# Splitting weights into high and low parts 1024 columns at a time instead of 512

## The chip, the cores and the metric

The kernel runs on one core of a Trainium2 chip. The metric is the device time of one execution in microseconds (us). Engines are named as in the profile: PE is TensorE (PEld its weight load), DVE is VectorE, ACT is ScalarE, POOL is GpSimd, SP is SyncE, on whose queue the loads of weights are issued.

## The reference, cut to what matters

Two blocks follow each other on 256 tokens of width 2048, all in float32. The first has two layers, each with a projection of the normed input into the columns of four mixers (gated linear attention, forgetting, differential and block attention), the mixers, and a projection back. The second has one layer with a modulated input projection for tokens and for a context, recurrent scans in both directions (RWKV-7 and a gated delta rule), a gated merge, and an MLP with squared ReLU. Nearly all of the multiplications are products of 256 tokens with large weights:

```python
def hybrid_layer(x, ...):                       # first block, two layers
    h = rms_norm(x, norm_g)
    p = split_columns(jnp.einsum("bsd,de->bse", h, w_in))
    ...                                         # four mixers
    return x + jnp.einsum("bse,ed->bsd", mixed, w_out)

def trunk_layer(x, ctx, c, c_ctx, ...):         # second block, one layer
    mod = jax.nn.silu(c) @ mod_w + mod_b
    h = modulate(rms_norm_2(x, norm1_w), sh1, sc1)
    p = h @ in_w
    ...                                         # scans, for tokens and context
    x = x + g1 * merge_branches(ya, yb, pg, up_a, up_b, out_w)
    x = x + g2 * squared_relu_mlp(modulate(rms_norm_2(x, norm2_w), sh2, sc2), mlp_w1, mlp_w2)

def squared_relu_mlp(h, w1, w2):
    return jnp.square(jax.nn.relu(h @ w1)) @ w2
```

## The kernel before, in words

Every float32 operand of a large product is split into a high part, rounded to float32r, and a low part, which is the rest. A product is then three matmuls: high weights with the high part of the activations (L171), high weights with the low part (L172), and low weights with the high part (L173). Where the two parts of the activations lie side by side (512 columns, in the output projection and in the second product of the MLP) the first two are one matmul (L166), and L167 is the one with the low weights. L203 to L205 are the same for outputs that stand as [token, feature].

Weights come from HBM as blocks of 128 x 2048. `load_w` loads a block as two tiles `wr` of 1024 columns, one DMA of 512 KB each, on SP's queue; there are three such buffers (WR). `pieces` makes of each 512 columns a high part `wh` by a copy on ACT (L230) and a low part `wl` by a subtraction on DVE (L231). There are five buffers of each kind (WH). A buffer of `wh` or `wl` becomes free when PE has done its last matmul with it, and a buffer of `wr` when the second subtraction from it is done. One `wr` holds eight slices of 128 columns, each the weights of one step over k; PE takes them in the order in which they were made.

The program is written stage by stage. A scheduler at build time lays out the order of the instructions of each engine; nothing is reordered when it runs. The loads and the split of weights are put AHEAD = 400 instructions before their place, so that they stand among other work on ACT and DVE. The stages of a run, by time, are: the first layer (to about 600 us) beside the modulation of the second block, whose steps use DVE (L901, L906), ACT (L911) and POOL (L912); the second layer (to about 1200); the scans, two at a time, with the projections of the second block between them (to about 2500); the merge and the start of the MLP (to about 2900); the rest of the MLP (to 3440); and the last norm. In the first two stages the softmax of the mixers stands on DVE too: L578 takes logits from PSUM, L529 row maxima, L426 to L430 rotate queries and keys.

Of the kernel before, what the change touches and what calls it, by code (L numbers as in the profile page):

```python
# [10 lines left out]
F32R = mybir.dt.float32r  # L11
# [5 lines left out]
PSUM = bass.MemoryType.PSUM  # L17
# [7 lines left out]
# how many instructions ahead of their place the operands of a projection are made  # L25
AHEAD = 400
# buffers of weights as they come, and of their parts
WR, WH = 3, 5
# buffers of 1 and 2 KB of the scans
N1, N2, NM = 6, 5, 4  # L30
# steps by which one scan runs ahead of the next
LEAD = 8
# banks of the projections, and of each of two scans
PP, S0, S1 = 3, 3, 2
# by how many instructions the scans go before the projections beside them
SCANS = 4000
# buffers of 2 KB of the scans, and of 4 KB of their inversions
NN, NL = 3, 3
# steps of the modulation by group of columns, for its first third and after
R0, R1, R2 = 3, 2, 3  # L40
# by how many instructions the parts of x go before their place
XO = (800, 300, 240, 200)
# groups of the modulation before the MLP; in the MLP, steps by pair of columns, from which pair on
MQ, MR, MS = 20, 3, 2
# the last product: on GpSimd or VectorE, and which rows
OUTS = ((0, 0, 1), (1, 12, 14), (0, 1, 3), (0, 3, 6), (0, 6, 9), (1, 14, 16), (0, 9, 12))
# how many of the context's activations are made early, buffers for the others
# [3 lines left out]
def bc(ap, n, axis):  # L51
    """ap with an axis of length n and step 0 put in at `axis`."""
    l = [list(x) for x in ap.ap]
    l.insert(axis, [0, n])
    return bass.AP(tensor=ap.tensor, offset=ap.offset, ap=l)


class Env:
    def __init__(self, tc, ctx):
# [8 lines left out]
        # which of two scans is being traced: each has its own banks  # L68
# [5 lines left out]
    def scr(self, shape, name):  # L74
        """A short-lived [128, up to 512]."""
        n = int(np.prod(shape[1:]))
        w, k = (512, 5) if n > 256 else (256, 3) if n > 64 else (64, 4)
        t = self.kp.tile([128, w], F32, name=name, tag="zsh" if w == 256 else f"scr{w}", bufs=k)[:shape[0], :n]
        return t.rearrange("p (a b) -> p a b", a=shape[1]) if len(shape) == 3 else t
# [10 lines left out]
    def consts(self):  # L90
# [7 lines left out]
        # tri[s, t] = 1 for s <= t, then ones: the running sums of two blocks of 128  # L98
        self.tri = c("tri", [128, 256])
        g.affine_select(self.tri, o, pattern=[[1, 256]], compare_op=ALU.is_ge, fill=0.0, base=0, channel_multiplier=-1)  # L100
        # fold[p, m] = 1 for p equal to m modulo 32
# [4 lines left out]
        # causal masks, 0 or -1e30: [q, key] of a block on the diagonal, and of the second row of blocks  # L106
# [4 lines left out]
    def level_masks(self):  # L111
        """uint8 masks [s, t] of pairs that a halving level joins: s in the left half, t in the
        right half of one block of 2b; the last is the diagonal."""
        nc, g = self.nc, self.nc.gpsimd
        self.lm = {}
        for b in (16, 8, 4, 2, 1):
            nb = 64 // b
            m = self.scr([128, 128], "lmf")
            # t in the right half of block j: start from ones on [j, half, i], zero on the left half
            mv = m.rearrange("p (n h i) -> p n h i", n=nb, h=2)  # L120
            g.memset(m, 0.0)
            # keep where 0 <= j*2b + b - 1 - s  (s <= last of left half) and s >= j*2b
# [10 lines left out]
    def load_w(self, dram):  # L133
        """One block of weights [128, 2048]; its high and low parts in four pieces each."""
        nc = self.nc
        out = []
        with self.tc.high_priority(offset=AHEAD):
            for j in range(2):
                w = self.wp.tile([128, 1024], F32, name="wr", tag="wr", bufs=WR)
                nc.sync.dma_start(w, dram[:, j * 1024:(j + 1) * 1024])  # L140
                for q in range(2):
                    out.append(self.pieces(w[:, q * 512:(q + 1) * 512]))
        return out

    def proj_t(self, h, dram, blocks, eat, nk=NK, w=T):
        """Two times 128 outputs, [feature, w columns of h], one after the other: eat(f, psum) for each."""
        n = 0
        for b in blocks:
            for hi, lo in self.load_w(dram[b]):
                for a in range(4):  # L150
# [10 lines left out]
    def mm3(self, o, hi, lo, h, k, nk):  # L161
        """o += what k adds; of 512 columns, the second half gets high times low."""
# [15 lines left out]
    def proj_k(self, h, dram, blocks, eat):  # L178
        """Two times 128 outputs, [feature, token], side by side, so that h is free by k as it ends:
        eat(f, psum); blocks of 1024 rows and 256 columns."""  # L180
        p = [self.pp()[:, :T] for _ in range(2)]
        k = 0
        for b in blocks:
            for hi, lo in self.load_w(dram[b]):
                for n in range(4):
                    sl = slice(n * 128, (n + 1) * 128)
                    self.mm3(p[n % 2], hi[:, sl], lo[:, sl], h, k + n // 2, NK)
                k += 2
# [4 lines left out]
    def proj_n(self, h, dram, tiles, eat, nk=NK):  # L193
        """512 outputs, [token, feature]: eat(block of tokens, psum)."""
# [4 lines left out]
        for ti in tiles:  # L199
            for hi, wlo in self.load_w(dram[ti]):  # L200
                for b in range(2):
                    x, xl = (h[i][:, k, b * 128:(b + 1) * 128] for i in range(2))
                    mm(p[b], x, hi, start=k == 0, stop=False)  # L203
                    mm(p[b], x, wlo, start=False, stop=False)
                    mm(p[b], xl, hi, start=False, stop=k == nk - 1)  # L205
                k += 1
# [4 lines left out]
    def proj_s(self, x, g, dram):  # L211
        """32 outputs of x * g, [feature, token]; dram [128, 16 x 32], g by feature. The sums over the k
        equal modulo 4 go to four groups of rows."""
# [12 lines left out]
    def pieces(self, sl):  # L226
        """(high, low) of weights [128, 512]."""
        hi = self.wp.tile([128, 512], F32R, name="wh", tag="wh", bufs=WH)
        lo = self.wp.tile([128, 512], F32R, name="wl", tag="wl", bufs=WH)
# [5 lines left out]
    def rsqrt(self, out, x, shape, tag, mult=1.0, eps=0.0):  # L235
        """out = (x * mult + eps) ** -0.5 by Newton's steps on VectorE."""
# [9 lines left out]
    def log1p_exp_neg_abs(self, out, x, shape, tag):  # L246
        """out = log(1 + exp(-|x|)); x in SBUF."""
# [34 lines left out]
    def total(self, acc, bank=None):  # L282
        """Sums over the partitions of acc [128, 256] by token, [128, 2]."""
# [10 lines left out]
    def rows(self, col, out=None, bank=None):  # L294
        """What is by token, [128, 2], as [128, 256] on all partitions."""
# [7 lines left out]
    def split(self, h, k, f):  # L303
        """h = (high, low) of float32 f at k."""
# [9 lines left out]
    def scaled(self, x, g):  # L314
        """(high, low) of x * g; g[:, k] by feature."""
# [7 lines left out]
def parts(tiles):  # L323
    """Of tiles [128, 2 x 256]: their high parts, their low parts, and both."""
# [3 lines left out]
class Slices:  # L328
    """Tiles [128, n] by k, indexed like one of [128, k, n]."""
# [8 lines left out]
def bc_like(ones, ap):  # L338
    """Ones in the shape of ap (three axes)."""
# [6 lines left out]
# ---------------------------------------------------------------- first block  # L346
# [3 lines left out]
# order of the blocks of columns in memory: name, columns, form  # L350
# [6 lines left out]
def first_layer(e, l, h, wd, small, pv, row, wa2, ba, rope, total, tick):  # L357
    """h: x with the norm's weights, total(): sums of squares by token; returns what w_out takes. The norm's
    factor by token goes on the projected columns. wd blocks of w_in, pv columns by feature; tick(): a
    piece of other work by each group of columns."""  # L360
# [15 lines left out]
    # small columns: gla_a in rows 0-15, fox_f in rows 16-19, of each of four parts  # L376
# [17 lines left out]
    def gate_t(name, out):  # L394
        """out[:, f, :] = 2 silu of the columns."""
# [25 lines left out]
    def rope_t(name, out, cos, sin, quads):  # L421
        for gi in range(2):
            def eat(f, ps, gi=gi):
# [3 lines left out]
                for q in quads:  # L427
                    # rows q..q+31 take rows q+32..q+63 and the other way round
# [7 lines left out]
    def out_norm(pt, blk, gcol, gate, k0):  # L436
        """pt: outputs of block blk of tokens [token, 4 x 128] in PSUM; rms norm by head, gate, and
        into mixed as [feature, token]."""
# [14 lines left out]
    # ---------------- gated linear attention  # L453
    def gla():
# [23 lines left out]
        for b in (128, 64, 32, 16, 8, 4, 2, 1, 0):  # L478
# [15 lines left out]
            # heads 2c in one bank, heads 2c + 1 in another: their rows of the array differ  # L494
            for r in range(2):
# [3 lines left out]
                # left halves of blocks that are not joined below 32 tokens  # L499
# [27 lines left out]
    def exps(S, n, m, lsum):  # L527
        """Row maxima, exponentials in place and their sums of S [128, 4, n]."""
# [5 lines left out]
    def logits(qT, kT, i, rows, S, post):  # L534
        """S[:, h, :] of block i of queries over the keys up to its end."""
# [1426 lines left out]
```

## Time and profile before

| | |
|---|---|
| time, median of three runs | 3481.61 us (3478.49 to 3493.04) |
| span of the profiled execution | 3473.1 us |
| PE busy | 3193.2 us, 92% of the span |
| DVE busy | 2646.0 us, 76% |
| ACT busy | 1716.1 us, 49% |
| subtractions of 512 columns (L231) | 1752, mean 763 ns |
| copies of 512 columns (L230) | 1752, mean 617 ns |
[...]

The profiled execution's span runs from its first to its last instruction. No time of that execution outside its span is listed; the median of the runs is 8.5 us longer than the span. Busy times are unions of an engine's instructions; they count an instruction to its end even where the next one has started.

### The profile page before, as it was taken

To read this page: it belongs to the slowest core of one execution; us is meant where nothing else is said; L and a number is where in the kernel's file an instruction comes from. 1 tells how busy PE (TensorE), PEld (TensorE's weight loads), DVE (VectorE), ACT (ScalarE), POOL (GpSimd) and SP (SyncE) were. 2 spreads that over 40 slices of the span, in tenths; PEclk is the share of its full clock that TensorE was granted. 3 is DMA by queue.
4 is the path that set the end of the run, shared out by engine and by line. 5 is a ranking of instruction groups with operands and counts; after the bars stand their busy time and mean duration, and the time that the engine had idled before them with its cause. 6 is when DMAs were issued, how large, how long until landed. Compare 5 with 4: busy or idle time off the path is not lost. (4 is left out here: it accounts for less than half of the span.)

```text
span 3473.1 us, 69690 instructions
## 1 busy us (share of the span) xinstructions
PE 3193.2 (92%) x25950; PEld 2968.2 (85%) x25950; DVE 2646.0 (76%) x5383; ACT 1716.1 (49%) x3403; POOL 899.8 (26%) x1254
## 2 busy tenths in 40 slices
PE   7898889998999989889798998998999999999998
PEld 6887869988789888879797898887898889899987
DVE  8998998799797688788688587566677886556665
ACT  5555555555554545444344344334354565445553
POOL 3544532133231033433303322312310330001000
PEclk9999999999999998989999999999999999999999
DMA  7666677786764564445545345355566775555554
GB/s 237 219 222 199 205 249 252 245 288 229 244 228 165 190 181 128 140 137 164 157 147 156 101 142 163 117 152 166 176 217 192 257 265 185 188 188 183 185 190 154
DMA packets 336096, 660.22 MB, mean 190 GB/s; under 512 B 99754, under 2 KB 163596, under 8 KB 335628
## 3 DMA queue, kind: packets, MB, share of 16 engines
q1 hardware_dynamic: 335756, 655.77, 59.2%
q8 instruction: 203, 3.33, 0.4%
q14 instruction: 137, 1.12, 0.1%
HBM read 621.41 MB, written 34.25 MB: 189 GB/s over the span
## 5 line engine op out<-in xcount | busy, mean ns | idle before, releaser
L231 DVE TENSOR_TENSOR wl<-wr,wh 128x512 fp32r<-128x512 f32 x1752 | 1318.4, 763 | 468.8 <-ACT wh L230 452.5
L230 ACT CAST wh<-wr 128x512 fp32r<-128x512 f32 x1752 | 1059.4, 617 | 967.9 <-PE pp L172 487.4
L173 PE MATMUL pp<-act,wl 128*128 128x256 f32 x3920 | 1147.6, 294 | 41.8 <-DVE wl L231 41.1
L171 PE MATMUL pp<-act,wh 128*128 128x256 f32 x3920 | 1144.0, 293 | 21.4 <-ACT wh L230 15.3
L172 PE MATMUL pp<-act,wh 128*128 128x256 f32 x3920 | 1140.2, 291 | 3.9 <-DVE act L963 3.8
L173 PEld LDWEIGHTS pp<-act,wl 128*128 128x128 f32 x3920 | 772.0, 197 | 65.3 <-DVE wl L231 57.2
L171 PEld LDWEIGHTS pp<-act,wh 128*128 128x128 f32 x3920 | 772.2, 197 | 34.2 <-ACT wh L230 18.6
L172 PEld LDWEIGHTS pp<-act,wh 128*128 128x128 f32 x3920 | 772.7, 197 | 12.9 <-DVE act L963 5.2
L912 POOL TENSOR_TENSOR macc<-macc,mw 128x512 f32<-128x512 f32 x232 | 342.2, 1475 | 631.6 <-ACT mw L911 400.9
L173 PE MATMUL pp<-mhi,wl 128*128 128x258 f32 x1024 | 293.5, 287 | 9.7 <-DVE wl L231 9.7
L171 PE MATMUL pp<-mhi,wh 128*128 128x258 f32 x1024 | 290.0, 283 | 0.1
L172 PE MATMUL pp<-mlo,wh 128*128 128x258 f32 x1024 | 288.3, 282 | 0.0
L911 ACT ACTIVATE mw<-mw,silu_c 128x512 f32<-128x512 f32 x232 | 167.6, 722 | 212.9 <-DMA mw<-in_mod_w 109.7
L166 PE MATMUL pp<-act,wh 128*128 128x512 f32 x752 | 266.1, 396 | 0.0
L167 PE MATMUL pp<-act,wl 128*128 128x256 f32 x768 | 212.8, 280 | 2.6 <-DVE wl L231 2.5
L173 PEld LDWEIGHTS pp<-mhi,wl 128*128 128x128 f32 x1024 | 193.0, 189 | 15.2 <-DVE wl L231 15.0
L171 PEld LDWEIGHTS pp<-mhi,wh 128*128 128x128 f32 x1024 | 194.6, 190 | 1.2 <-ACT wh L230 0.5
L172 PEld LDWEIGHTS pp<-mlo,wh 128*128 128x128 f32 x1024 | 194.6, 190 | 0.1
L1134 POOL TENSOR_TENSOR own<-own,sub 128x30 f32<-128x30 f32 (+4 forms) x360 | 175.0, 486 | 26.8
L1133 POOL TENSOR_TENSOR sub<-X,own 128x30 f32<-128x30 f32 (+4 forms) x360 | 172.7, 480 | 27.8 <-POOL own L1128 0.4
L166 PE MATMUL pp<-u,wh 128*128 128x512 f32 x480 | 168.2, 392 | 0.0
L166 PEld LDWEIGHTS pp<-act,wh 128*128 128x128 f32 x752 | 141.2, 188 | 31.4
(528 smaller groups left out, 4991.8 us busy)
## 6 DMA issues: line engine op xcount, KB each, us to landing
wr<-in_in_w SPq DMA_DIRECT2D x252, 512.0 KB, 5.0
wr<-in_w SPq DMA_DIRECT2D x240, 512.0 KB, 4.4
mw<-in_mod_w SPq DMA_DIRECT2D x192, 512.0 KB, 5.0
wr<-in_w1m SPq DMA_DIRECT2D x128, 512.0 KB, 3.7
wr<-in_w2m SPq DMA_DIRECT2D x128, 512.0 KB, 3.6
wr<-in_wo SPq DMA_DIRECT2D x64, 512.0 KB, 4.3
wr<-in_out_w SPq DMA_DIRECT2D x32, 512.0 KB, 4.3
wr<-in_up_a SPq DMA_DIRECT2D x16, 512.0 KB, 4.1
```

Source lines behind the costliest of these rows:

```text
L166: mm(o, hi, h[2][:, k, :], start=k == 0, stop=False)
L167: mm(o[:, :T], lo, h[0][:, k, :], start=False, stop=False)
L171: mm(o, hi, h[0][:, k, :], start=k == 0, stop=False)
L172: mm(o, hi, h[1][:, k, :], start=False, stop=False)
L173: mm(o, lo, h[0][:, k, :], start=False, stop=k == nk - 1)
L230: self.nc.scalar.copy(hi, sl)
L231: self.nc.vector.tensor_tensor(lo, sl, hi, op=SUB)
L911: nc.scalar.activation(w[:, j], w[:, j], AF.Copy, scale=sc)
L912: nc.gpsimd.tensor_tensor(accs["c0"], accs["c0"], w[:, j], op=ADD)
L1133: g.tensor_tensor(t, bc(Xm[:, j + 1:, j], w, 2), bc(Om[:, j, :w], n, 1), op=MUL)
L1134: g.tensor_tensor(Om[:, j + 1:, :w], Om[:, j + 1:, :w], t, op=ADD)
```

## The change

`pieces` is called once for each `wr` instead of twice: one copy and one subtraction of 128 x 1024 take the place of two of 128 x 512. Buffers of parts are now 1024 columns wide, three for the high parts and two for the low ones. Before, the parts took 2 x 5 x 2 KB of each partition, now 3 x 4 KB + 2 x 4 KB, which is the same 20 KB. The three helpers that multiply walk over eight slices of a piece instead of four. The matmuls, their number and the DMAs stay as they are. All the other lines of the file's diff are comments that are gone; one line more at the top moves most line numbers up by one (L231 becomes L232).

```diff
-WR, WH = 3, 5
+WR, WH, WL = 3, 3, 2
...
     def load_w(self, dram):
...
                 nc.sync.dma_start(w, dram[:, j * 1024:(j + 1) * 1024])
-                for q in range(2):
-                    out.append(self.pieces(w[:, q * 512:(q + 1) * 512]))
+                out.append(self.pieces(w))
...
     def proj_t(self, h, dram, blocks, eat, nk=NK, w=T):
...
-                for a in range(4):
+                for a in range(8):
...
     def proj_k(self, h, dram, blocks, eat):
...
-                for n in range(4):
+                for n in range(8):
...
-                k += 2
+                k += 4
...
     def proj_n(self, h, dram, tiles, eat, nk=NK):
...
-            for hi, wlo in self.load_w(dram[ti]):
-                for b in range(2):
+            for two, twolo in self.load_w(dram[ti]):
+                for n in range(2):
+                    hi, wlo = (x[:, n * 512:(n + 1) * 512] for x in (two, twolo))
+                    for b in range(2):
...
     def pieces(self, sl):
...
-        hi = self.wp.tile([128, 512], F32R, name="wh", tag="wh", bufs=WH)
-        lo = self.wp.tile([128, 512], F32R, name="wl", tag="wl", bufs=WH)
+        hi = self.wp.tile([128, 1024], F32R, name="wh", tag="wh", bufs=WH)
+        lo = self.wp.tile([128, 1024], F32R, name="wl", tag="wl", bufs=WL)
         self.nc.scalar.copy(hi, sl)
         self.nc.vector.tensor_tensor(lo, sl, hi, op=SUB)
```

The order of the instructions shows how the subtractions now stand among DVE's other work. The first place is the softmax of the forgetting attention in the first layer (L578 and L529 in the kernel before, L579 and L530 in the changed one), with the modulation's L901 and the rotation of the next queries (L426 to L430) beside it. Before, on DVE:

```order
L231 TENSOR_TENSOR wl<-wr,wh 128x512 x2
L901 SCALAR_TENSOR_TENSOR mps<-mw,silu_cc,mps 128x512
L578 SCALAR_TENSOR_TENSOR S_2341<-sm,fb_1553 128x512
L901 SCALAR_TENSOR_TENSOR mps<-mw,silu_cc,mps 128x512
L578 SCALAR_TENSOR_TENSOR S_2357<-sm,Sd 128x512
L426 TENSOR_TENSOR qT<-pp,rope 128x256
...
L231 TENSOR_TENSOR wl<-wr,wh 128x512
L529 TENSOR_REDUCE sm_m<-S_2341 128x4
L578 SCALAR_TENSOR_TENSOR S_2357<-sm,Sd 128x512
L231 TENSOR_TENSOR wl<-wr,wh 128x512
```

And in the changed kernel, at the same place of the program on DVE, from one subtraction to the next:

```order
L232 TENSOR_TENSOR wl<-wr,wh 128x1024
L900 TENSOR_SCALAR mps<-mw,silu_cc 128x512
L902 SCALAR_TENSOR_TENSOR mps<-mw,silu_cc,mps 128x512
L579 SCALAR_TENSOR_TENSOR S_2181<-sm,fb_1457 128x512
L902 SCALAR_TENSOR_TENSOR mps<-mw,silu_cc,mps 128x512
L530 TENSOR_REDUCE sm_m<-S_2181 128x4
L579 SCALAR_TENSOR_TENSOR S_2197<-sm,Sd 128x512
L902 SCALAR_TENSOR_TENSOR mps<-mw,silu_cc,mps 128x512
...
L579 SCALAR_TENSOR_TENSOR S_2197<-sm,Sd 128x512
L427 TENSOR_TENSOR qT<-pp,rope 128x256
...
L530 TENSOR_REDUCE sm_m<-S_2197 128x4
L232 TENSOR_TENSOR wl<-wr,wh 128x1024
```

The subtractions that cut this work into three parts have moved out of it: all three L579, both L530 and four steps of the modulation now stand between two subtractions.

The second place is a little earlier on DVE, where the forgetting attention's biases are made (L611, four instructions each for the two blocks of queries; L612 in the changed kernel). Before:

```order
L611 SCALAR_TENSOR_TENSOR fb_1553<-fb_1553,ft,cm 128x128 x4
L231 TENSOR_TENSOR wl<-wr,wh 128x512
L901 SCALAR_TENSOR_TENSOR mps<-mw,silu_cc,mps 128x512
L242 TENSOR_TENSOR nwz<-nwy 128x2
L611 SCALAR_TENSOR_TENSOR Sd<-Sd,ft,cm 128x256 x4
L231 TENSOR_TENSOR wl<-wr,wh 128x512
```

And in the changed kernel:

```order
L232 TENSOR_TENSOR wl<-wr,wh 128x1024
L612 SCALAR_TENSOR_TENSOR fb_1457<-fb_1457,ft,cm 128x128 x4
L243 TENSOR_TENSOR nwz<-nwy 128x2
L612 SCALAR_TENSOR_TENSOR Sd<-Sd,ft,cm 128x256 x4
L399 TENSOR_TENSOR gate<-pp,rstd 128x256
L232 TENSOR_TENSOR wl<-wr,wh 128x1024
```

The subtraction between the two groups of four has moved ahead of both.

## Rows read from the trace of the kernel before

**Rows 1.** Windows: length; busy of PE, PEld, DVE, ACT, POOL; clock; DMA share, GB/s.

```profile
20.00:600.00 580.00, 507.55 (x3620) 460.68 (x3619) 536.14 (x862) 328.93 (x637) 244.99 (x170) 0.96 0.68 223
600.00:1200.00 600.00, 566.23 (x4241) 527.31 (x4240) 489.57 (x875) 320.06 (x635) 141.06 (x103) 0.98 0.68 229
1200.00:2500.00 1300.00, 1171.26 (x11463) 1102.12 (x11461) 957.66 (x2430) 554.61 (x1176) 395.74 (x833) 0.94 0.50 148
2500.00:2900.00 400.00, 380.85 (x2851) 358.90 (x2851) 307.81 (x589) 215.57 (x431) 82.58 (x75) 1.00 0.70 227
2900.00:3440.00 540.00, 540.00 (x3622) 497.42 (x3622) 325.05 (x562) 275.97 (x483) 22.28 (x36) 1.00 0.58 187
```

**Rows 2.** The same windows, the subtractions of line L231 alone.

```profile
20.00:600.00 580.00, 255.22 (x289) 0.96 0.68 223
600.00:1200.00 600.00, 265.25 (x341) 0.98 0.68 229
1200.00:2500.00 1300.00, 340.47 (x483) 0.94 0.50 148
2500.00:2900.00 400.00, 184.56 (x244) 1.00 0.70 227
```

**Rows 3.** Waits of PE from 0 to 600 us: total, times, longest.

```profile
PE pp L173 <- DVE wl L231: 31.2, 36, 3.7
```

**Rows 4.** Waits of PE from 600 to 1200 us.

```profile
PE pp L173 <- DVE wl L231: 10.5, 13, 1.9
```

**Rows 5.** Waits of PE from 1200 to 2500 us.

```profile
PE sm L1160 <- ACT xb L1148: 54.4, 11, 9.7
```

**Rows 6.** Waits of PE from 2500 to 2900 us.

```profile
PE pp L173 <- DVE wl L231: 9.7, 16, 1.2
```

**Rows 7.** Groups by line and shape, whole span: count, busy us, mean ns.

```profile
L231 DVE TENSOR_TENSOR wl<-wr,wh 128x512 fp32r<-128x512 f32 x1752 | 1318.4, 763 | 468.8 <-ACT wh L230 452.5 <-PE pp L173 4.9 <-ACT zsh L1065 0.3
...
L230 ACT CAST wh<-wr 128x512 fp32r<-128x512 f32 x1752 | 1059.4, 617 | 967.9 <-PE pp L172 487.4 <-PE pp L166 149.4 <-DMA wr<-in_w 94.8
...
L529 DVE TENSOR_REDUCE sm_m<-S 128x4 f32<-128x1024 f32 x6 | 7.2, 1204 | 0.0
...
L529 DVE TENSOR_REDUCE sm_m<-S 128x4 f32<-128x512 f32 x6 | 4.1, 676 | 0.0
```

**Rows 8.** Timeline of DVE, 13 to 17 us: start, us, instructions merged.

```profile
14.46 1.88 DVE L231 TENSOR_TENSOR wl<-wr,wh 128x512 fp32r<-128x512 f32 x3
16.26 0.87 DVE L319 SCALAR_TENSOR_TENSOR act<-x,pv,act 128x256 fp32r<-128x256 f32 x2
```

**Rows 9.** Timeline of DVE, 630 to 632 us.

```profile
630.06 1.43 DVE L306 TENSOR_TENSOR act<-x,act 128x256 fp32r<-128x256 f32 x4
631.40 0.69 DVE L231 TENSOR_TENSOR wl<-wr,wh 128x512 fp32r<-128x512 f32 x1
```

**Rows 10.** Timeline of DVE, 2952 to 2955 us, in the MLP's second product.

```profile
2952.51 0.69 DVE L231 TENSOR_TENSOR wl<-wr,wh 128x512 fp32r<-128x512 f32 x1 [0.69 <-ACT wh L230]
2953.90 0.69 DVE L231 TENSOR_TENSOR wl<-wr,wh 128x512 fp32r<-128x512 f32 x1 [0.69 <-ACT wh L230]
```

**Rows 11.** Timeline of DVE, 264 to 269 us, in the first layer's softmax.

```profile
264.23 0.74 DVE L901 SCALAR_TENSOR_TENSOR mps<-mw,silu_cc,mps 128x512 f32<-128x512 f32 x1
264.89 0.68 DVE L578 SCALAR_TENSOR_TENSOR S<-sm,fb 128x512 f32<-128x512 f32 x1
265.49 0.74 DVE L901 SCALAR_TENSOR_TENSOR mps<-mw,silu_cc,mps 128x512 f32<-128x512 f32 x1
...
268.92 0.69 DVE L231 TENSOR_TENSOR wl<-wr,wh 128x512 fp32r<-128x512 f32 x1
```

**Rows 12.** Timeline of DVE, 238 to 245 us, where the biases are made.

```profile
238.92 2.15 DVE L611 SCALAR_TENSOR_TENSOR fb<-fb,ft,cm 128x128 f32<-128x128 f32 x4
...
242.33 2.67 DVE L611 SCALAR_TENSOR_TENSOR Sd<-Sd,ft,cm 128x256 f32<-128x256 f32 x4
244.92 0.68 DVE L231 TENSOR_TENSOR wl<-wr,wh 128x512 fp32r<-128x512 f32 x1
```

More of the change, by code (lines that the diff above doesn't have):

```diff
@@ L199, in proj_n @@
         for ti in tiles:
-            for hi, wlo in self.load_w(dram[ti]):
-                for b in range(2):
[L202 to L206, printed above, removed]
+            for two, twolo in self.load_w(dram[ti]):
+                for n in range(2):
+                    hi, wlo = (x[:, n * 512:(n + 1) * 512] for x in (two, twolo))
+                    for b in range(2):
+                        x, xl = (h[i][:, k, b * 128:(b + 1) * 128] for i in range(2))
+                        mm(p[b], x, hi, start=k == 0, stop=False)
+                        mm(p[b], x, wlo, start=False, stop=False)
+                        mm(p[b], xl, hi, start=False, stop=k == nk - 1)
+                    k += 1
         with self.tc.high_priority(offset=AHEAD):
```

## The prediction, on record before the changed kernel's time was known

> **What bounds the kernel now.** I read the windows by stage first, then PE's waits in each stage, then the shape of single subtractions in the timeline. The windows [rows 1] show three kinds of stage. In the first (20 to 600 us) DVE is busy for 536 of 580 us, 92%, and PE for 508: DVE is nearly the bound, and PE loses 72 us. From 600 to 1200 PE is busy for 566 of 600 us and DVE for 490, so both are close. From 2900 on PE is busy for all of 540 us and DVE for 60%: there PE alone sets the time. In the scans (1200 to 2500) PE loses 129 us, but its longest wait is for a matrix inversion that comes back by way of ACT, 54.4 us [rows 5], and not for weights. What PE waits for low parts of weights is listed by stage: 31.2 us in the first 600 us [rows 3], 10.5 in the next 600 [rows 4], 9.7 in the merge [rows 6]. That is 51 us in all, 1.5% of the span, and it is the most that faster splitting could give back directly.
>
> **What the change removes.** 1752 subtractions become 876 of twice the width [rows 7]; the copies on ACT likewise, but ACT is busy for at most 57% of any stage [rows 1], so I count nothing for it. What a merged pair saves on DVE has two bounds. Back to back, three subtractions of 512 start 0.60 us apart (16.26 less 14.46, by three), and four of the same kind with 256 columns 0.335 us apart [rows 8, 9]. So 256 columns cost 0.265 us, one of 1024 would take 0.60 + 0.53 = 1.13 us, and a pair saves 0.07 us. That is the lower bound. By whole durations, a DVE instruction over 1024 columns lasts 1204 ns and over 512 lasts 676 [rows 7], which leaves 148 ns that do not grow with the width: the upper bound, for places where DVE stands between two dependent steps. I take 0.07, since the stage in which it counts has DVE busy almost without gaps.
>
> [...]
>
> The pairs by stage are half the counts of line L231 [rows 2]. First stage: 144 pairs by 0.07 is 10 us (by 0.148, 21), nearly all of it time, as DVE is the bound. 600 to 1200: 170 pairs, 12 us of DVE, but PE waits only 10.5 us there; I take 4. Scans: 241 pairs, 17 us of DVE off the path; I take 2. Merge: 122 pairs, 9 us; PE waits 9.7; I take 4. MLP: nothing, PE has no gap. The sum is 20 us, between 0 and 21 + 10.5 + 9.7 = 41. The subtractions of the first stage last 883 ns on average (255.22 us by 289) against 0.69 alone [rows 2, 10], beside POOL's 170 instructions [rows 1]. That surcharge is 0.19 us by 289, 56 us. POOL's instructions stay, so I leave it in; if it went by instruction and not by time, half of it, 28 us, would go too.
>
> **What the change adds.** A wait: the subtraction now needs a low buffer that PE freed, and there are two. In the MLP PE takes 1.39 us for 512 columns, as the period of the subtractions there shows [rows 10]. Before, a buffer freed at the end of one piece serves the fifth piece after it, needed 4 x 1.39 = 5.6 us later; copy and subtraction take 0.62 + 0.69 [rows 7, 10], so some 4.2 us are to spare. Now a low buffer freed by one piece of 1024 serves the second after it, needed 2.78 us later, of which the subtraction takes 1.13 to 1.2: 1.6 us to spare. The three high buffers leave more (5.6 less about 1.1 for the copy), so the low ones are what binds. In the MLP DVE idles 0.69 us before each subtraction [rows 10], and 1.6 us are enough: no loss in the 540 us.
>
> Where DVE has more than about 1.6 + 1.6 = 3.2 us of other work between two subtractions, PE now runs dry, and the order shows such places. In the first softmax the work between two subtractions was 4.7 us (264.23 to 268.92) [rows 11]. In the changed order two more steps of the modulation (about 0.65 us each), one more L578 (0.60) and both row maxima (0.6 and 1.13 by the same pitch) join it: 8.3 us in one piece. PE then has at most two pieces ready, 5.6 us, with 1.1 us more for the next subtraction: some 3 us of waiting more than before. There are eight such softmaxes in the two layers (one each for two mixers, two for the differential one). At the biases two groups of 2.15 and 2.67 us [rows 12], parted by a subtraction before, now stand together; there is one such place in each layer, 2 us each. That makes 28 us. As PE also has matmuls of the mixers to do in these stretches, which need no weights, I take 22. The bounds are 0 (all of it falls under such matmuls) and 63, if each of the 314 pairs of the first two stages lost 0.2 us. Behind a subtraction that waits for PE stand the mixers' and the modulation's instructions on DVE, and ACT and POOL wait for those.
>
> In the scans a subtraction holds DVE for 1.13 us at a time instead of 0.60, with steps of the recurrences behind it. The trace has no row for that; the bounds are 0 and 0.1 us for each of 241 pairs, 24 us. I take 4, since PE's large wait there is the inversion's [rows 5]. The loads of weights wait for the subtraction that frees a `wr`; they start later by about as much as the subtraction does, 1.5 us, and still have three pieces of PE's time, 8.3 us. I count nothing.
>
> **The sum.** -20 + 22 + 4 = +6 us on a span of 3473.1. The median of the runs shown lies 8.5 us above that span; I add the same: 3488 us, 0.2% above 3481.6. A measurement of this kernel can tell about 0.5%, 17 us, from no change, so the forecast is no difference that can be told.
>
> **The rivals.** *The relief decides.* If the scheduler's order keeps PE fed in spite of two low buffers (the loss is 5 us) and a pair saves its full 0.148 us where DVE is the bound, the gain is the 41 us above: 3481.6 - 36 = 3446. For it speaks DVE's 92% in the first stage; against it, that PE waits for low parts for only 51 us in all, and the overlap of neighbours in the timeline. [...] *The two low buffers decide.* The loss is at its bound of 63 us, in the softmax and bias stretches of the first 1200 us, against a relief of 20 and with 4 for the scans: 3481.6 + 47 = 3529. For it speaks that DVE is the tighter engine there, so that work banked ahead in five buffers is what carries PE over such stretches; against it, that with weights often late already the bank is seldom full. It decides from the point at which PE's waits for low parts in the first 1200 us pass 65 us, from 42 now. *The loads come late.* If the wait for a freed `wr` grew past the 8.3 us, PE would wait for high parts; 20 us in the stages with the highest DMA share (0.70 [rows 1]), 3505. Against it speaks the margin.
>
> **How the numbers follow.** The forecast, with its own range of 3466 to 3498, has a chance of 0.42; the relief 0.25; the low buffers 0.29; the loads 0.04. Faster by over 0.5% is the second case, 0.25; slower the last two, 0.33; the rest, 0.42, is within 0.5%. The range reaches to the second and third case and a little past them, since both bounds are open: 3440 to 3540.
>
> **What the changed profile would show.** Right: subtractions of 1024 columns that last 1.2 us alone; DVE's busy time 60 to 130 us lower, near 2550; the stage from 2900 on of the same length with PE at 100%; PE's waits for low parts in the first 1200 us between 35 and 65 us, with the longest of them, 3 to 5 us, at the softmaxes; DVE waiting for PE before subtractions, where it now waits for ACT. Wrong: subtractions far from 1.2 us, PE with gaps in the MLP, waits for high parts or for loads that grow, or a scan stage that is longer by more than 25 us.

## The result, and the profile after

The changed kernel takes 3528.51 us (median of four runs, 3525.22 to 3542.15), the kernel before 3482.32 (four runs). The ratio is 1.0136, interval 1.0115 to 1.0157: slower by 46 us. That lies in the range of 3440 to 3540, but the forecast, no difference that can be told, was not met. The size is that of the second rival, the two low buffers, yet not at the place that the rival named: that its 3529 us is met to the microsecond is luck.

The page of the changed kernel, busy time by engine:

```profile
PE 3210.0 (91%) x25950; PEld 2980.2 (85%) x25950; DVE 2506.8 (71%) x4507; ACT 1599.8 (45%) x2527; POOL 959.4 (27%) x1254
```

DVE is busy for 139.2 us less than before, PE for 16.8 more. The two groups that answer to [rows 7] (count, busy us, mean ns, idle time before them):

```profile
L232 DVE TENSOR_TENSOR wl<-wr,wh 128x1024 fp32r<-128x1024 f32 x876 | 1139.7, 1302 | 359.6 <-PE pp L166 140.4 <-PE pp L172 63.6 <-ACT wh L231 50.7
L231 ACT CAST wh<-wr 128x1024 fp32r<-128x1024 f32 x876 | 917.4, 1048 | 1115.9 <-PE pp L171 377.8 <-DMA wr<-in_w2m 172.1 <-DMA wr<-in_in_w 146.4
```

In [rows 7] a subtraction waited for the copy on ACT (452.5 us) and hardly for PE (4.9). Now it waits for PE, L166 and L172, which is to free a low buffer; and the copies wait more for loads.

Where the 46 us went is seen when both kernels are cut at the same work: behind 2100, 4200 and 4800 of the 6752 matmuls with a low part, which are the end of the first two layers (but for the second one's output projection, which stands in the next window), the end of the scans, and a place in the MLP behind the merge. Windows cut there, before and then after (columns as in [rows 1]):

```profile
0.00:1107.00 1107.00, 995.58 (x7325) 912.65 (x7325) 974.46 (x1620) 612.13 (x1183) 384.93 (x294) 0.97 0.70 231
1107.00:2513.00 1406.00, 1268.71 (x12137) 1193.01 (x12136) 1030.34 (x2603) 608.64 (x1304) 406.88 (x848) 0.94 0.51 151
2513.00:2750.00 237.00, 227.79 (x1622) 212.59 (x1620) 181.58 (x371) 122.95 (x254) 33.14 (x30) 0.99 0.66 212
2750.00:3473.00 723.00, 701.11 (x4874) 649.91 (x4872) 459.63 (x792) 372.41 (x662) 74.89 (x83) 0.99 0.60 196
```

```profile
0.00:1102.00 1102.00, 990.78 (x7334) 907.78 (x7335) 910.89 (x1328) 580.34 (x891) 416.68 (x294) 0.98 0.70 232
1102.00:2554.00 1452.00, 1288.50 (x12135) 1208.70 (x12134) 1007.75 (x2339) 574.05 (x1042) 422.98 (x848) 0.92 0.49 147
2554.00:2801.00 247.00, 229.72 (x1614) 213.07 (x1613) 171.47 (x295) 114.17 (x177) 40.10 (x30) 0.98 0.64 202
2801.00:3524.00 723.00, 700.98 (x4875) 650.65 (x4873) 416.69 (x548) 331.27 (x418) 79.59 (x83) 0.99 0.61 196
```

The first two layers are 5 us shorter and the MLP is the same to 1 us. The scans are 46 us longer and the merge 10 to 11. In the scans PE is busy for 20 us more with the same matmuls, at a granted clock of 0.92 instead of 0.94, and idle for 26 us more (1452 less 1288.5, against 1406 less 1268.7).

PE's waits for parts of weights in the changed kernel, first two layers and then scans (total, times, longest):

```profile
PE pp L172 <- DVE wl L232: 47.5, 52, 3.3
PE pp L205 <- DVE wl L232: 19.7, 18, 3.3
PE pp L170 <- ACT wh L231: 17.2, 15, 3.1
```

```profile
PE sm L1161 <- ACT xb L1149: 56.7, 8, 11.5
PE pp L170 <- ACT wh L231: 33.2, 8, 7.4
PE pp L172 <- DVE wl L232: 11.1, 16, 2.0
```

And in the scans of the kernel before:

```profile
PE pp L171 <- ACT wh L230: 6.6, 3, 3.8
PE pp L173 <- DVE wl L231: 3.2, 5, 1.2
```

The wait for the inversion that answers to [rows 5] has hardly moved. What is new in the scans is PE waiting for *high* parts: eight waits, 33.2 us, up to 7.4 each. Together the two waits grew by 34.5 us, more than the 26 of PE's idle time. Three of the eight, 18.6 us, stand in the output projection. One of these, in the changed kernel's timeline, SP's queue from 1225 to 1246 us:

```profile
1225.02 0.33 SPq L140 DMA_DIRECT2D wr<-in_wo  x1
...
1230.84 4.04 SPq L1423 DMA_DIRECT2D aup<-in_aup  x1
1234.99 0.58 SPq L140 DMA_DIRECT2D wr<-in_wo  x1
```

ACT and DVE in the same stretch:

```profile
1229.38 1.05 ACT L231 CAST wh<-wr 128x1024 fp32r<-128x1024 f32 x1 [1.14 <-PE pp L171]
...
1242.99 1.04 ACT L231 CAST wh<-wr 128x1024 fp32r<-128x1024 f32 x1 [11.85 <-DMA wr<-in_wo]
```

```profile
1229.54 1.22 DVE L232 TENSOR_TENSOR wl<-wr,wh 128x1024 fp32r<-128x1024 f32 x1
...
1232.30 1.22 DVE L232 TENSOR_TENSOR wl<-wr,wh 128x1024 fp32r<-128x1024 f32 x1
```

And PE:

```profile
1236.43 0.28 PE L171 MATMUL pp<-act,wh 128*128 128x256 f32 x1
1244.09 0.58 PE L170 MATMUL pp<-act,wh 128*128 128x256 f32 x1 [7.38 <-ACT wh L231]
```

Read from the end: PE stands for 7.38 us until a copy has been made; the copy stood for 11.85 us until its load had landed; the load was issued at 1234.99, 10 us after the one ahead of it, though the buffer it fills (the three are used in turn) was free when the subtraction of 1229.54 ended at 1230.76. It stood on SP's queue behind another DMA that held the queue for 4.04 us, and then took 8 us more. So here the late subtraction is only a part; the rest is what stands behind a load that has missed its turn. The next wait, 50 us later, shows another thing that can stand there:

```profile
1280.20 0.32 SPq L1906 DMA_DIRECT2D x1d<-xold  x1
1288.94 0.32 SPq L1140 DMA_DIRECT2D ivb<-own  x1
1289.36 0.37 SPq L140 DMA_DIRECT2D wr<-in_wo  x1
```

```profile
1294.98 0.58 PE L170 MATMUL pp<-act,wh 128*128 128x256 f32 x1 [7.13 <-ACT wh L231]
```

The buffer of this load was free at 1281.39, but its place on SP's queue is behind a DMA of the matrix inversion (`ivb<-own`), which waited for POOL until 1288.9. When each load of the trace is put beside its copy, and beside the subtraction that frees its buffer, six of the eight waits (25 of the 33 us) have a load that was issued 1.7 to 9.5 us after its buffer had come free. What a stall like this does to PE's clock, in windows of the changed kernel before the gap, after it, and next:

```profile
1231.20:1236.20 5.00, 5.00 (x44) 4.92 (x43) 4.93 (x12) 0.00 (x0) 0.00 (x0) 1.00 0.16 48
...
1244.20:1248.20 4.00, 4.00 (x19) 4.00 (x20) 3.53 (x11) 3.40 (x9) 0.00 (x0) 0.50 0.93 273
1248.20:1254.00 5.80, 5.80 (x44) 5.54 (x44) 4.09 (x11) 3.58 (x7) 2.92 (x9) 0.91 0.94 284
```

Before the gap PE's granted clock is 1.00; after 7.4 us without work it is 0.50 in the 4 us that follow. The other four of these waits that last over 3 us are each followed by 4 us at 0.50 as well. Such a stall costs more than its own length: PE starts 19 matmuls in these 4 us, and 44 in the 5 us before the gap.

### The profile page after: what moved, and what is told of

It is laid out like the page before. It is cut to its first block, busy times and chain, and to the rows that moved or that the text cites. A ratio compares the mean times of both kernels' runs of the same rounds, so it can differ in the third digit from the quotient of the medians.

```text
span 3524.0 us, 66710 instructions
## 1 busy us (share of the span) xinstructions
PE 3210.0 (91%) x25950; PEld 2980.2 (85%) x25950; DVE 2506.8 (71%) x4507; ACT 1599.8 (45%) x2527; POOL 959.4 (27%) x1254
## 5 line engine op out<-in xcount | busy, mean ns | idle before, releaser
L231 ACT CAST wh<-wr 128x1024 fp32r<-128x1024 f32 x876 | 917.4, 1048 | 1115.9 <-PE pp L171 377.8
L232 DVE TENSOR_TENSOR wl<-wr,wh 128x1024 fp32r<-128x1024 f32 x876 | 1139.7, 1302 | 359.6 <-PE pp L166 140.4
L172 PE MATMUL pp<-act,wl 128*128 128x256 f32 x3920 | 1141.8, 295 | 55.7 <-DVE wl L232 55.1
L170 PE MATMUL pp<-act,wh 128*128 128x256 f32 x3920 | 1141.0, 293 | 51.4 <-ACT wh L231 50.4
L172 PEld LDWEIGHTS pp<-act,wl 128*128 128x128 f32 x3920 | 768.0, 197 | 84.0 <-DVE wl L232 73.7
L913 POOL TENSOR_TENSOR macc<-macc,mw 128x512 f32<-128x512 f32 x232 | 354.8, 1529 | 511.5 <-ACT mw L912 358.2
L172 PE MATMUL pp<-mhi,wl 128*128 128x258 f32 x1024 | 284.3, 285 | 6.7 <-DVE wl L232 6.5
L166 PE MATMUL pp<-act,wl 128*128 128x256 f32 x768 | 214.2, 282 | 5.5 <-DVE wl L232 5.3
L1135 POOL TENSOR_TENSOR own<-own,sub 128x30 f32<-128x30 f32 (+4 forms) x360 | 193.9, 539 | 26.9
L172 PEld LDWEIGHTS pp<-mhi,wl 128*128 128x128 f32 x1024 | 189.8, 188 | 9.5 <-DVE wl L232 8.7
```

Of the source, the lines that this page charges most:

```text
L166: mm(o[:, :T], lo, h[0][:, k, :], start=False, stop=False)
L170: mm(o, hi, h[0][:, k, :], start=k == 0, stop=False)
L172: mm(o, lo, h[0][:, k, :], start=False, stop=k == nk - 1)
L231: self.nc.scalar.copy(hi, sl)
L232: self.nc.vector.tensor_tensor(lo, sl, hi, op=SUB)
L913: nc.gpsimd.tensor_tensor(accs["c0"], accs["c0"], w[:, j], op=ADD)
```

## The experiments

Theory: two low buffers are too few; a subtraction waits for PE, the loaded buffer (`wr`) it reads stays taken, the next load, copy and high part come late, and PE stands. Rivals: the wide instruction itself; the loads alone; late low parts alone, without the loads. The runs of the kernel before on the chips of the experiments had medians of 3474.64 (first four, seven runs), 3477.74 (next four, seven) and 3479.26 us (last four, 21); ratios are against these, and since the chips differ it is ratios that compare, not medians. The table sets each kernel's profiled execution beside that of the kernel before, by the same cuts (us; the rest is the MLP). Its last column is the sum of PE's waits for high and low parts in the scans, 9.8 us in the kernel before. In half, wide_ctrl, wide_low3, wide_wr4 and narrow_squeezed, 64 to 320 fewer of the matmuls without parts of weights, the scans' own, are done by the cut behind the scans (6540 to 6796 from the start, against 6860 before): of their columns for the scans and the merge only the sum counts.

| kernel | median us | ratio | first layers | scans | merge | waits for parts |
|---|---|---|---|---|---|---|
| changed | 3528.51 | 1.0136 | -5 | +46 | +11 | 44.3 |
| half | 3520.07 | 1.0132 | +9 | +11 | +23 | 43.6 |
| narrow_low3 | 3534.86 | 1.0178 | +1 | +62 | 0 | 54.2 |
| wide_ctrl | 3559.80 | 1.0243 | +8 | +46 | +30 | 30.4 |
| wide_low3 | 3499.68 | 1.0081 | -29 | +12 | +35 | 3.2 |
| wide_wr4 | 3532.21 | 1.0153 | +1 | +29 | +35 | 10.2 |
| wide_wh4 | 3556.55 | 1.0225 | +8 | +70 | +7 | 45.1 |
| narrow_squeezed | 3526.95 | 1.0143 | +4 | +23 | +25 | 1.2 |
| narrow_4_6 | 3495.51 | 1.0049 | -2 | +34 | -4 | 11.6 |
| two_pools | 3498.01 | 1.0050 | 0 | +24 | +2 | 9.1 |
| wide_first | 3490.13 | 1.0030 | -4 | +20 | 0 | 12.8 |
| wide_after | 3533.50 | 1.0149 | +3 | +62 | -3 | 59.2 |
| wide3_first | 3470.01 | 0.9971 | -24 | +24 | -1 | 13.0 |

The last column parts the kernels in two. Those with two wide or three narrow low buffers in the scans, and three buffers of loads, wait 30 to 59 us for parts; all the others, with other orders of instructions among them, 1 to 13.

**half: the changed kernel's buffers, the old width of instructions.**

```diff
-        self.nc.scalar.copy(hi, sl)
-        self.nc.vector.tensor_tensor(lo, sl, hi, op=SUB)
+        for q in range(2):
+            c = slice(q * 512, (q + 1) * 512)
+            self.nc.scalar.copy(hi[:, c], sl[:, c])
+            self.nc.vector.tensor_tensor(lo[:, c], sl[:, c], hi[:, c], op=SUB)
```

> Buffers as in the change (1024 columns wide, three high, two low), but each piece is made by two copies and two subtractions of 512 columns, as before. Three theories of the 46 us that the change costs (3482 to 3528), nearly all of it between 1100 and 2630 us, in the scans and the merge. Depth: two low buffers leave the subtraction 2.8 us of PE's time instead of 5.6, and it comes late among the steps of the scans; then this kernel keeps the loss and also pays back the fixed part of the instructions, 3530 to 3545. Width: one subtraction holds DVE for 1.2 us in front of the scans' steps; then most of the loss goes, 3480 to 3495. Loads: a buffer of loaded weights comes free only after the late subtraction, and the next load is late; this goes with depth here, 3530 to 3545.

3520.07 us, ratio 1.0132 (1.0105 to 1.0159), 10 us under the range of depth and far above that of width: the loss stays with narrow instructions, so in sum it does not come from their width. The table has more in it: the wide instructions are worth 14 us in the first two layers (-5 against +9), and these are gone again by the end of the merge, though another order alone moves as much (two_pools, below).

**narrow_low3: the kernel before with three low buffers instead of five.**

```diff
-WR, WH = 3, 5
+WR, WH, WL = 3, 5, 3
...
-        lo = self.wp.tile([128, 512], F32R, name="wl", tag="wl", bufs=WH)
+        lo = self.wp.tile([128, 512], F32R, name="wl", tag="wl", bufs=WL)
```

> The kernel before, with pieces of 512 columns and five high buffers, but three low buffers instead of five. A low buffer freed by one piece then serves the third after it, needed 2 x 1.39 = 2.8 us of PE's time later, as in the change; instructions are narrow and buffers are freed by 512. Depth: 3510 to 3540, and the loss again between 1100 and 2630 us. Width: 3480 to 3490, no difference. Loads: as depth, since the subtraction that frees the load is as late as in the change.

3534.86 us, ratio 1.0178 (1.0152 to 1.0204). With fewer low buffers as the only edit the loss is there again, all of it in the scans.

**wide_ctrl and wide_low3: the changed kernel with a third low buffer.** It needs 4 KB, which are taken from the context's early activations (EK) and the scans' small buffers (N1); wide_ctrl has only that squeeze.

```diff
-WR, WH, WL = 3, 3, 2
+WR, WH, WL = 3, 3, 3
-N1, N2, NM = 6, 5, 4
+N1, N2, NM = 5, 5, 4
-EK, HM = 8, 4
+EK, HM = 6, 4
```

> The changed kernel with 3 KB less elsewhere (six instead of eight early activations of the context, and five instead of six buffers of 1 KB of the scans), to stand beside the next one, which needs that room. All theories: within 15 us of the changed kernel, 3515 to 3545.

> The kernel with 3 KB less elsewhere, with a third low buffer of 1024 columns. Depth: a low buffer freed by one piece serves the third after it, needed 5.6 us later, as before the change: 35 to 60 us less than its control beside it, so about 3475 to 3490. Width: no difference to the control, within 10 us. Loads: as depth, since the load's buffer is freed earlier too.

wide_ctrl 3559.80 us, ratio 1.0243 (1.021 to 1.0277): the squeeze cost more than was expected. wide_low3 3499.68, ratio 1.0081 (1.0054 to 1.0108): the third low buffer gives back 60 us, the upper end of what depth gave. The copies' waits for loads in wide_low3's scans:

```profile
ACT wh L231 <- DMA wr<-in_in_w: 15.8, 5, 6.0
ACT wh L231 <- DMA wr<-in_wo: 9.6, 3, 6.4
```

and in wide_ctrl's:

```profile
ACT wh L231 <- DMA wr<-in_in_w: 104.6, 42, 11.9
ACT wh L231 <- DMA wr<-in_wo: 26.0, 10, 9.2
```

The number of buffers for loads is the same in both. In narrow_low3, where only the low buffers were touched, the copies' waits for loads in the scans are 210 us against 69 before. That the loads come late is an effect of the low buffers: shown.

**wide_wr4 and wide_wh4: the same 4 KB elsewhere**, as a fourth buffer of loads or of high parts; N1 and EK are as in wide_ctrl.

```diff
-WR, WH, WL = 3, 3, 2
+WR, WH, WL = 4, 3, 2
```

```diff
-WR, WH, WL = 3, 3, 2
+WR, WH, WL = 3, 4, 2
```

> The kernel wide_ctrl (changed kernel in the tighter memory, 3559.8 us, ratio 1.0243) with one thing more: four buffers of loaded weights (wr) instead of three, 4 KB, the same 4 KB that the third low buffer took in wide_low3 (3499.7, ratio 1.0081). Theory A, the chain: a subtraction that waits for one of two low buffers holds a wr, so the next load and the next high part come late, and PE waits for the high part. A fourth wr takes the load out of the chain but leaves the subtraction where it is: the copies on ACT no longer wait for DMA (under 60 us against 247 in wide_ctrl), PE waits for high parts under 20 us against 44.5, and the time lies 15 to 40 us under wide_ctrl, 3520 to 3545, ratio 1.013 to 1.020. Theory B, the loads alone: 3495 to 3515, as much as the third low buffer. Theory C, the low part itself is what comes late and the loads do not matter: within 10 us of wide_ctrl, 3550 to 3570.

> The kernel wide_ctrl with a fourth buffer of high parts instead, again 4 KB. By all of the theories on the low buffers the high parts are not what is short: a fourth one can't be used while the subtraction behind it waits for a low buffer, since the wr is not freed. Within 10 us of wide_ctrl: 3550 to 3570, ratio 1.022 to 1.027. Rival: any 4 KB more in the ring of weights helps as much as any other, 3500 to 3520.

wide_wr4 3532.21 us, ratio 1.0153 (1.0136 to 1.0170); wide_wh4 3556.55, ratio 1.0225 (1.0199 to 1.0251). A fourth high buffer does nothing; a fourth load buffer gives back 0.0090 of the ratio where the low buffer gave 0.0162. PE's waits in the scans of wide_wr4:

```profile
PE pp L172 <- DVE wl L232: 9.7, 12, 2.3
PE pp L170 <- ACT wh L231: 0.5, 1, 0.5
```

and of wide_ctrl:

```profile
PE pp L170 <- ACT wh L231: 22.7, 5, 7.4
PE pp L172 <- DVE wl L232: 7.7, 12, 2.1
```

The waits for high parts are gone, those for low parts as they were. So in the scans the chain through the loads is what cost PE its waits for high parts. From 1600 us to the cut the two have nearly the same order (82 of PE's 8235 matmuls stand elsewhere), and there wide_wr4 makes 13 us of its gain in the scans. By the whole times the chain is about half of the low buffers' price (each of the two differences is known to some 0.004); in the first two layers (8 of the 37 us between wide_ctrl and wide_low3) it is little, and there the low part itself is late.

**narrow_squeezed: the kernel before in the tighter memory** (only EK and N1 as above).

> The kernel before (512 columns, five and five buffers) in the tighter memory of wide_ctrl and wide_low3 (six instead of eight early activations of the context, five instead of six small buffers of the scans). The tighter memory cost the changed kernel 3559.8 against 3528.5, 0.0107 of the ratio. If it costs the kernel before as much, 3512, ratio 1.011, then the three wide low buffers at 1.0081 are no slower than the five narrow ones. If it costs nothing here, 3470 to 3480, the tighter memory hurts only where low buffers are short, and three wide low buffers still lose 25 us to five narrow ones.

3526.95 us, ratio 1.0143 (1.0123 to 1.0162). The squeeze alone costs the kernel before no less than it cost the changed one (0.0107), more than either expectation, nearly all of it behind the first two layers. In this memory three wide buffers of each kind (1.0081) beat five narrow ones, but they hold 24 KB and not 20; the lead, 33 us, is made in the first two layers.

**narrow_4_6: four high and six low buffers of 512.**

```diff
-WR, WH = 3, 5
+WR, WH, WL = 3, 4, 6
```

> The kernel before with four buffers of 512 columns for high parts and six for low ones, the same 20 KB. If low parts are what runs short, six of them against five gain up to 15 us or change nothing, 3460 to 3485. If high parts are as short as low ones, it loses as a buffer less did: some 20 to 30 us, 3495 to 3505, as three low buffers instead of five lost 60.

3495.51 us, ratio 1.0049 (1.0034 to 1.0064). At the lower end of the second expectation. But PE waits for parts hardly more than before (11.6 us), and 17 us are what another order alone costs in two_pools: that the missing high buffer is the cause is not shown.

**two_pools, wide_first, wide_after, wide3_first: another width in each block.** The parts have one pool in the first block and another after it; the width and the buffers are chosen for each.

```diff
-WR, WH, WL = 3, 3, 2
+WR = 3
+PARTS = (1024, 3, 2), (512, 5, 5)
...
+    e.width = PARTS[0]
+    with tc.tile_pool(name="parts1", bufs=1) as e.qp:
...
+    e.width = PARTS[1]
+    with tc.tile_pool(name="parts2", bufs=1) as e.qp:
```

This is wide_first; two_pools has (512, 5, 5) twice, wide_after the two the other way round, wide3_first (1024, 3, 3), (512, 5, 5) and EK = 6.

> Control: the kernel before (512 columns, five and five buffers throughout), with the parts of weights in one pool for the first block (both of its layers but for the last product) and another for all that follows, at the same addresses. The first parts of the second pool wait until PE has used those of the first at the same place, which they did before too. Same time as the kernel before: ratio 0.997 to 1.003.

> 1024 columns with three high and two low buffers in the first block, as in the changed kernel, and 512 columns with five and five in all that follows, as before. The traces put all of the loss in the scans and the merge (5 us gained by the end of the two layers, 50.8 lost by the merge's end). If it is the buffers there, this kernel keeps the small gain: ratio 0.995 to 1.002. Rival: the loss stems from the first block, which leaves the scans a worse start (later loads, another order): ratio 1.007 to 1.014.

> The other half: 512 columns with five and five buffers in the first block, 1024 with three high and two low in all that follows. If the loss is in the scans and the merge, it is all here: ratio 1.012 to 1.018, 42 to 62 us over the kernel before. By the rival, 0.997 to 1.004.

> 1024 columns with three high and three low buffers in the first block, paid by six instead of eight early activations of the context, then 512 with five and five. The kernel wide_low3 stood 29 us ahead of the kernel before at the end of the two layers, and lost it in the scans and the merge, as narrow_squeezed did with as tight a memory there (five small buffers of the scans instead of six), which this kernel does not have. If so, the 29 us stay, but for some that the scans lose: 3445 to 3465, ratio 0.990 to 0.997. Rival: the scans wait for something else (an inversion, a chain of steps) and the lead is lost to it: ratio 0.997 to 1.003.

two_pools 3498.01 us, ratio 1.0050 (1.0034 to 1.0066): missed, the control is not neutral. wide_first 3490.13, 1.0030 (1.0017 to 1.0043). wide_after 3533.50 (five runs, one of them 4986.5 us), 1.0149 (1.0128 to 1.0169, of the other four). wide3_first 3470.01, 0.9971 (0.9958 to 0.9984). wide_first lies between its two expectations, wide_after in the first, wide3_first at the edge of its rival. Against two_pools, wide_first is 0.0020 faster and wide_after 0.0099 slower: the loss is made behind the first block. wide3_first is the only kernel faster than the one before, by 9 us, and 28 faster than two_pools; of the 24 us that it is ahead after the first two layers, the scans take all. The windows of two_pools show where its control lost:

```profile
0.00:1107.00 1107.00, 1001.23 (x7326) 916.58 (x7327) 973.46 (x1620) 612.17 (x1183) 382.38 (x294) 0.97 0.70 231
1107.00:2537.00 1430.00, 1283.36 (x12139) 1207.01 (x12138) 1030.36 (x2606) 610.12 (x1304) 406.46 (x848) 0.92 0.50 149
```

With the same width and number of buffers the scans take 24 us more: PE busy 14.7 us longer at a mean granted clock of 0.92 instead of 0.94, and 9 us more idle. What differs is the order that the scheduler lays out there: up to 1150 us the trace has the instructions of each engine in the order of the kernel before, behind it not. PE's waits for parts do not grow by it (9.1 us against 9.8). So an amount of some 25 us in the scans says little of a mechanism, and the growth of the waits for parts does. Of the buffers' loss behind the first two layers there are five pairs, fewer low buffers against more, summed to the end: 56 us (changed), 40 (half), 63 (narrow_low3), 27 (wide_ctrl against wide_low3) and 32 (wide_after against two_pools). The sign is always the same; the size is not known to better than this spread. The first three are against the kernel before, whose order is a good one: two_pools, wide_first, wide3_first and narrow_4_6, which have low buffers enough there, lose 19 to 26 us against it behind the first two layers too. In the last two pairs neither kernel has that order; they put the buffers' own share at some 30 us (an estimate from these two).

## Why the prediction was wrong, step by step

The measured time lies in the stated range because this had been drawn over the rivals; the forecast itself and the places of its terms were wrong.

**The step that failed** is the one on the loads: "they start later by about as much as the subtraction does, 1.5 us, and still have three pieces of PE's time, 8.3 us. I count nothing." In the scans neither number holds. For the eight waits of PE, the subtraction that frees the buffer started 2.5 to 4.9 us after its copy; the load then stood on SP's queue for up to 9.5 us more behind other DMAs, and took 4.2 to 13.3 us from issue to copy, which the step did not count. PE's waits for high parts in the scans grew by 26.6 us, where the step counted nothing. The rival of late loads named the right wait, PE's for high parts, but at 20 us and as a matter apart from the low buffers; its 3505 us is not the sum of its terms either, as 20 us on top of the forecast are 3508. wide_low3 shows that it is their effect: with the third of them the two rows shown of the copies' waits for loads fall from 130.6 us to 25.4. The merge and the scans together were forecast at 2 us of gain (4 of loss less 2 and 4 of relief) and came out at 56 us of loss. With it fell the second rival's place: it put the loss into the first 1200 us, because DVE is fullest there. That DVE and PE are less full in the scans was taken for slack; it is not. As I read it, the work comes in bursts there around chains of dependent steps; what the rows show is that loads stand behind such a step's DMA on SP's queue, and that PE's granted clock is 0.50 in the 4 us after each of the five of these waits that last over 3 us.

**The relief** came out at its size, 10 and 4 us for the first two layers against 14 us by the traces (-5 of the changed kernel, +9 of half, which differ in the width of the instructions and in the order that the scheduler makes of it). That is in part luck: a pair saved over twice the 0.07 us that was counted, and less of it became time than was assumed; and the squeeze of wide_ctrl alone moves the first layers by as much (+8 against -5). The 4 and 2 us for the merge and the scans are not to be seen: there the wide instructions lose about 15 us against half, though that is within what the order alone moves.

**Durations.** Subtractions in the MLP's second product answer to [rows 10]; DVE's timeline of the changed kernel:

```profile
2983.32 1.23 DVE L232 TENSOR_TENSOR wl<-wr,wh 128x1024 fp32r<-128x1024 f32 x1 [1.56 <-PE pp L166]
2986.12 1.23 DVE L232 TENSOR_TENSOR wl<-wr,wh 128x1024 fp32r<-128x1024 f32 x1 [1.57 <-PE pp L166]
```

1.23 us every 2.80, and 1.56 us idle until PE frees a buffer: the 2.78, 1.2 and 1.6 us of the forecast. The two low buffers bind, and there it costs nothing. DVE's busy time fell by 139.2 us for 876 pairs, 0.159 us a pair: a little over the upper bound of 0.148, and not the 0.07 that I took, and more than the 60 to 130 us that were named as a sign. The median duration of the 876 subtractions is 1224 ns, that of the 1752 of 512 columns before 691 ns. But the 314 pairs of the first two stages at 0.159 would be 50 us, and 14 were gained: time off a busy engine is not time off the span.

**The low buffers in the first two layers** were put at 22 us of loss and cost 9 (half against before). The mechanism is the one named, at the softmax that answers to [rows 11]: DVE's timeline of the changed kernel from one subtraction to the next, and PE behind it.

```profile
249.18 1.21 DVE L232 TENSOR_TENSOR wl<-wr,wh 128x1024 fp32r<-128x1024 f32 x1
...
255.57 0.75 DVE L902 SCALAR_TENSOR_TENSOR mps<-mw,silu_cc,mps 128x512 f32<-128x512 f32 x1 [3.13 <-DMA mw<-in_mod_w]
...
262.42 1.22 DVE L232 TENSOR_TENSOR wl<-wr,wh 128x1024 fp32r<-128x1024 f32 x1
```

```profile
263.69 0.58 PE L172 MATMUL pp<-act,wl 128*128 128x256 f32 x1 [2.92 <-DVE wl L232]
```

PE waits 2.92 us, forecast as some 3. The stretch without a subtraction is 12 us and not 8.3, since the modulation's load comes late in it; PE still loses no more, as it has matmuls of the mixers and the modulation to do, 3.9 us of them from 250.2 us on. At the biases of the first layer, the other place that was named, nothing more was lost: PE's waits for parts are 3.7 us from 225 to 250 us, and 4.2 before (232 to 250).

PE's waits for low parts in the first two layers are 47.5 us at L172, inside the 35 to 65 that was named; with L205, 67.2, against 50.4 before. The MLP's stage kept its length, as forecast. Of the signs of an error that were named, two came: waits for high parts that grow, and a scan stage more than 25 us longer.

**What stays open** is how the loss in the scans parts into the buffers' waits and the order: 26 us idle and 20 us of slower PE are measured, and a change of the order alone makes 9 and 15. The growth of the waits for parts is the buffers'; whose the slower PE is was not parted. Why the merge loses 11 us in the changed kernel, and none in narrow_low3 and wide_after, was not tried.

## What to carry to other kernels

Where one engine makes and another uses, the buffer that is freed last holds all those before it: ask of each wait that a smaller ring adds not only who waits for its result, but which input buffer stays taken meanwhile, which load that holds, and what stands before the load on its queue. Fewer and larger buffers in the same memory save instructions, and lose banked work; here that loss showed in the stage where the loads' queue also carries the steps of other work, not where the engine is busiest on average. And before 20 us are put down to a mechanism in a stage whose order a scheduler lays out, run a control that changes the order alone.

## What was not expected of the hardware

After a gap of 7.4 us PE ran at a granted clock of 0.50 in the next 4 us, where it had 1.00 before the gap, and of the 46 us lost in the scans 20 are PE busy for longer with the same matmuls, at 0.92 instead of 0.94. The eight loads `aup`, 256 KB each, held SP's queue for 4.0 to 7.1 us each (4.3 to 6.9 in the kernel before), where an issue of a weight load of 512 KB mostly holds it for 0.33.
